# The opening of a hybrid attention and expert kernel: another order of loads, column products and table

## Chip, cores and metric

One core of one Trainium2 chip. The metric is the device time of one execution in microseconds; three runs of the kernel before gave 1021.66, 1022.80 and 1024.69, median 1022.8.

## The reference, cut to what matters

```python
def reference(x, c, w_ada, b_ada, norm_attn, ..., norm_final):
    mod = jnp.einsum('bd,lde->lbe', jax.nn.silu(c), w_ada) + b_ada[:, None, :]
    for l in range(DEPTH):                       # DEPTH = 1
        sh1, sc1, g1, sh2, sc2, g2 = jnp.split(mod[l], 6, axis=-1)
        h = modulate(rms_norm(x, norm_attn[l]), sh1, sc1)     # h*(1+scale)+shift
        x = x + g1[:, None, :] * hybrid_mixer(h, w_in[l], w_out[l], rel_bias)
        h = modulate(rms_norm(x, norm_ffn[l]), sh2, sc2)
        x = x + g2[:, None, :] * peer_ffn(h, peer_wq[l], peer_subkeys[l], peer_u[l], peer_v[l])
    return rms_norm(x, norm_final)
```

x is 256 rows of 1024 values; `w_ada` is 1024 x 6144, its six parts of 1024 columns are shift, scale and gate of the two halves (parts 0 to 5). `hybrid_mixer` projects h with one matrix to queries, keys and values of 16 heads and a small indexer, adds a bias of relative position, and takes softmax attention: 8 heads over a causal block, 8 heads over the keys that the indexer selects. `peer_ffn` is an expert layer with 16384 one-neuron experts.

## The kernel before, in words

x is held transposed: 8 tiles of 128 features by 256 tokens (`xT`). Products that need full precision are made from two halves of each operand, a rounded high part (ScalarE, L106) and the rest as low part (VectorE, L108), in three matmuls (`mm3`, L125 to L127). Weight tiles of 128x1024 (512 KB) come one after the other through four `raw` buffers (`load_next`, L94), in the order of the list `seq`; all loads are issued by SyncE. `take` gives out the next split tile, and `ahead` keeps loads and splits in front of it.

**The opening** (up to `start.close()`) stands in a region of manual schedule: there each engine issues its instructions, SyncE its DMAs too, in the order in which the code emits them. Behind it a scheduler orders the instructions by the order of emission and its own estimate of when they are ready; the order of the attention's parts is the string ORDER (A projects queries and keys of a pair of heads, S makes its scores and softmax, B multiplies with the values, I, N and T are the indexer's projections, norm and selection, V the second half of the values, Dk accumulates part k of `w_ada` and Ek makes its columns).

In the opening:
- SyncE loads small tables, x, two weight tiles, the 8 chunks of the scale part (part 1) of `w_ada` (L158), two weight tiles and the 8 chunks of the shift part (part 0), through 11 buffers, then the value tiles.
- ScalarE squares x (L236), TensorE sums over the features (L237), and VectorE with ScalarE makes rstd (L190 to L196).
- The scale vector is a product of silu(c) with 8 chunks of 128 rows. Chunks 0, 2 and 4 are multiplied on TensorE into rows (`ada_rows`, L300), copied (L303) and turned into columns by products with one value (L309). The other chunks are scaled and added on VectorE (`ada_dve`, L208 and L210), and `ada_end` (L317, L320) sums them over the partitions by products with a single column of ones, and adds the bias into `mod`. Products of ones with ones (`busy`, L257) are filler; their result is not used.
- `early_split` (L322) splits the first four weight tiles (two pairs of heads): two of them before rstd, two after `xh_all`.
- `xr_all` (L350) multiplies x by rstd; `xh_all` (L353 to L357) scales it into high part xh and low part xl. `early_mm` makes the projections of the first four tiles from them, still without the shift (96 products, L125 to L127), tiles 0 and 1 by turns of halves, then tiles 2 and 3.
- The shift vector (part 0) is accumulated wholly on VectorE in two halves of columns; after each half `ada_end`, and `sh_half` (L365 to L368) adds the shift to get h, as hh and hl. `early_shift` (L337) and `early_cols` (L342 to L345) make the correction of the early projections.
- `vproj_steps` (L274) multiplies four value tiles with h, each with the three products of `mm3`; the second half of them stands behind the opening.
- The bias of relative position: a one-hot product (L391), copied into `fr` (L394), written to DRAM (`frd`, L397, by SyncE behind all loads of `w_ada`), and read back as the table `bias` of 2 MB (L440) after `early_cols`, into a pool that takes the memory of the opening's weights.

After that A0 and A1 only copy the early projections out (L453), and S0 starts with scores (L494) and the sum with the bias (L504).

Of the kernel before, what the change touches and what calls it, by code (L numbers as in the profile page):

```python
# [7 lines left out]
FT = mybir.dt.float32  # L8
# [8 lines left out]
T = 256  # L17
# [14 lines left out]
NTAIL = 125  # L32
ORDER = "D2 S0 S1 I N B0 A2 T A3 B1 S2 D4 A4 S3 B2 E2 A5 S4 B3 A6 S5 E4 D3 A7 V B4 S6 B5 S7 B6 E3 B7"
EARLY = 4
BUSY0 = 13
BUSY1 = 2
BUSY2 = 4
ADA_PE = {(1, 0): (0, 2, 4), (1, 1): (0, 2, 4), (0, 0): (), (0, 1): ()}


@with_exitstack
def hybrid_kernel(ctx, tc, io, out):
# [11 lines left out]
    def bank(tag, bufs=1):  # L54
        return psum.tile([128, 512], FT, tag=tag, name=tag, bufs=bufs)
# [62 lines left out]

    def take():
        ahead(5, 3)  # L120
        at["use"] += 1
        return parts.pop(at["use"] - 1)
# [15 lines left out]
    start = ctx.enter_context(ExitStack())  # L138
    start.enter_context(tc.manual_schedule())
    w0_stack = ctx.enter_context(ExitStack())  # L140
    w0 = pool("w0", stack=w0_stack)
# [57 lines left out]
    def rows_rsqrt_steps(ps, n):  # L199
        r3 = [pf.tile([128, T], FT, tag="r3", name="r3", bufs=4) for _ in range(3)]  # L200
        return rsqrt_steps(ps[:, :T], *r3, 1.0 / n)

    def rows_rsqrt(ps, n):
        return list(rows_rsqrt_steps(ps, n))[1]

    def ada_step(acc, w, c, first):
# [8 lines left out]
    def ada_sum(part):  # L215

        acc = acc_tile()
        for c in range(8):
            ada_step(acc, ada_load(part, c), c, c == 0)
        return acc  # L220
# [13 lines left out]
    def square_sum(ms, x, c):  # L234
        sq = pf.tile([128, T], FT, tag="sq", name="sq", bufs=4)
        nc.scalar.activation(sq, x[:, c, :], AF.Square)  # L236
        nc.tensor.matmul(ms[:, :T], ones, sq, start=(c == 0), stop=(c == 7))  # L237
# [36 lines left out]
    def vproj_steps(g):  # L274
        pv = [bank_a() for _ in range(2)]
        for k in range(4):
            hi, lo = take()
            for c2 in range(2):
                c = 2 * k + c2
                w = slice(c2 * 512, c2 * 512 + 512)  # L280
                for tt in range(2):
                    ts = slice(tt * 128, tt * 128 + 128)
                    mm3(pv[tt], hh[:, c, ts], hl[:, c, ts], hi[:, w], lo[:, w], c == 0, c == 7)
            yield None
        for tt in range(2):
            nc.scalar.activation(v[:, tt, g * 512:(g + 1) * 512], pv[tt], AF.Copy)
# [7 lines left out]
    def ada_rows(part, half, box):  # L294
# [12 lines left out]
        for q in range(4):  # L307
            w = slice(q * 128, q * 128 + 128)
            nc.tensor.matmul(cols[:, q:q + 1], row[:, w], ones[0:1, 0:1], start=(q == 0),  # L309
                             stop=(q == 3 and len(chunks) == 8), skip_group_check=True)  # L310
        yield None

    def ada_end(part, half, cols):

        if len(ADA_PE[part, half]) < 8:
            for q in range(4):
                nc.tensor.matmul(cols[:, q:q + 1], (acc1 if part else acc0)[:, (half * 4 + q) * 128:(half * 4 + q + 1) * 128],  # L317
                                 ones[:, 0:1], start=(q == 0 and not ADA_PE[part, half]), stop=(q == 3), skip_group_check=True)
        s = slice(part * 8 + half * 4, part * 8 + half * 4 + 4)
        nc.vector.tensor_tensor(mod[:, s], cols[:, 0:4], bada[:, s], op=OP.add)  # L320

    def early_split():  # L322
        k = len(early_w)
        early_w.append(split(raws.pop(k), nc.vector, ehi[:, k, :], elo[:, k, :]))
        at["split"] += 1
        at["use"] += 1
# [19 lines left out]

    def xr_all():

        for c in range(8):
            nc.vector.tensor_tensor(xa[:, c, :], xT[:, c, :], rstd, op=OP.mult)  # L350

# [21 lines left out]

    box = {(1, 0): lambda: bank("c1")[:, 0:4], (1, 1): lambda: bank_a()[:, 4:8]}
    r10, r11 = ada_rows(1, 0, box), ada_rows(1, 1, box)
# [11 lines left out]
    for _ in range(3):  # L387
        next(r10)
        next(r11)
    fps = bank_a()  # L390
    nc.tensor.matmul(fps[:16, :256], rbT, oh, start=True, stop=True)  # L391
    fr = pf.tile([16, 384], FT, name="fr")
    nc.gpsimd.memset(fr, NEG)
    nc.scalar.activation(fr[:, :256], fps[:16, :256], AF.Copy)  # L394
    dp = pool("dp", space=bass.MemoryType.DRAM)
    frd = dp.tile([16, 384], FT, name="frd")
# [37 lines left out]

    at_stack = ctx.enter_context(ExitStack())
    pa = pool("pa", stack=at_stack)
    bias = pa.tile([128, 16, T], FT, name="bias")
    fa = frd[:]
    for g in range(2):
        nc.sync.dma_start(bias[:, 8 * g:8 * g + 8, :],  # L440
                          bass.AP(tensor=fa.tensor, offset=fa.offset + 8 * g * 384, ap=[[1, 128], [384, 8], [1, T]]))

# [15 lines left out]
    def proj_mm():  # L458
# [5 lines left out]
        return ps  # L464


# [81 lines left out]
    def indexer_norm():  # L548
        ik = IX["ik"]
        sq = pf.tile([128, T], FT, tag="sq", name="sq", bufs=4)  # L550
        nc.scalar.activation(sq[:64, :], ik[:64, :], AF.Square)
# [78 lines left out]
    for db in range(8):  # L630
        hi, lo = take()
        ps = bank_a()
        for c in range(8):
# [3 lines left out]
                                       op0=OP.mult, op1=OP.add)  # L637
        sq = pf.tile([128, T], FT, tag="sq", name="sq", bufs=4)
        nc.scalar.activation(sq, xT[:, db, :], AF.Square)
# [411 lines left out]
```

## Time and profile before

| | |
|---|---|
| median of 3 runs | 1022.8 us |
| the profiled execution's own time | 1022.12 us |
| its span in the trace | 1020.2 us |
| mean granted TensorE clock | 0.986 |
| TensorE busy | 979.2 us, 96% of the span |
| VectorE busy | 779.2 us, 76% |
| ScalarE busy | 634.8 us, 62% |
| DMA, mean over the span | 191 GB/s |

One execution is profiled; its trace lists each instruction with its start and duration, in microseconds from the span's start. PE is TensorE, PEld its loading of weights, DVE VectorE, ACT ScalarE, POOL GpSimd, SP SyncE; a q behind the name is the engine's instruction queue. Lnnn is the line of the kernel. An fp32 matmul shows as two passes. "[1.03 <-DVE s L505]" says that the engine stood idle 1.03 us before the instruction and what ended the wait. PEclk is the clock that TensorE was granted, as a share of 2.4 GHz.

### The profile page before, as it was taken

The numbers are of one execution on the slowest core, as the hardware profiler recorded it, in microseconds if no ns is written. First come the engines' busy times: TensorE is split into PE (matmuls) and PEld (weight loads), VectorE is DVE, ScalarE is ACT, GpSimd is POOL, SyncE is SP. The second block draws the span as 40 slices with busy tenths as digits, with TensorE's granted clock in tenths as the row PEclk, the third lists the DMA queues.
The fourth block names the chain that finished last, engine by engine and source line by source line (L and its number), as shares of the span: only waits on it lengthen the run. The fifth ranks groups of instructions, "written<-read, shape, count | busy, mean of one in ns | idle before, by whom it ended". The sixth has DMA issues, their size and how long they took to land.

```text
span 1020.2 us, 16221 instructions
## 1 busy us (share of the span) xinstructions
PE 979.2 (96%) x5691; PEld 832.9 (82%) x5691; DVE 779.2 (76%) x1601; ACT 634.8 (62%) x1419; POOL 20.8 (2%) x62
## 2 busy tenths in 40 slices
PE   8899799899899999999999999999999999999996
PEld 5768687899678788888888888887888888888885
DVE  5768996789999988888889898767555555555556
ACT  3556476455556599988988888544544555545443
POOL 0000010002100000000000000000000000000000
PEclk9799999999999999999999999999999999999999
DMA  8588574555356555555555555678665665565551
GB/s 347 214 288 301 157 245 140 170 173 162 122 165 187 173 178 165 166 166 166 166 168 168 164 169 167 216 254 283 210 198 191 190 199 189 193 199 188 199 191 63
DMA packets 54996, 195.15 MB, mean 191 GB/s; under 512 B 6097, under 2 KB 8193, under 8 KB 54530
## 3 DMA queue, kind: packets, MB, share of 16 engines
q1 hardware_dynamic: 54626, 192.80, 58.2%
q10 hardware_dynamic: 288, 1.31, 0.3%
q8 instruction: 45, 0.74, 0.3%
q14 instruction: 37, 0.30, 0.1%
HBM read 191.97 MB, written 2.12 MB: 190 GB/s over the span
## 4 chain that ended last, share of the span: by engine, by line
PE 62%; DVE 8%; DMA 2%; ACT 2%; issue 1%; DVEq 0%; ACTq 0%
PE c L898 11%; PE c L126 10%; PE c L125 10%; PE c L127 10%; PE pa L898 8%; PE c L899 6%; PE pa L899 4%; DVE lo L108 2%; PE pb L855 1%; PE pb L856 1%; DMA raw<-w_ada 1%; DMA raw<-V 1%; ACT hi L106 1%; DVE gt L905 1%; ACT ol L848 0%
## 5 line engine op out<-in xcount | busy, mean ns | idle before, releaser
L108 DVE TENSOR_TENSOR lo<-raw,hi 128x1024 fp32r<-128x1024 f32 x300 | 366.4, 1223 | 168.7 <-ACT hi L106 167.8
L106 ACT ACTIVATE hi<-raw 128x1024 fp32r<-128x1024 f32 x303 | 320.3, 1058 | 228.4 <-PE c L127 151.6
L898 PE MATMUL c<-h,hi 128*128 128x512 f32 x608 | 218.2, 399 | 1.2 <-ACT hi L106 1.2
L126 PE MATMUL c<-lo,w 128*128 128x512 f32 x509 | 198.6, 390 | 1.2 <-DVE lo L108 1.2
L125 PE MATMUL c<-hi,w 128*128 128x512 f32 x509 | 198.5, 390 | 0.0
L127 PE MATMUL c<-hi,w 128*128 128x512 f32 x509 | 197.9, 389 | 0.0
L899 PE MATMUL c<-h,lo 128*128 128x256 f32 x608 | 158.4, 281 | 5.1 <-DVE lo L108 5.1
L898 PE MATMUL pa<-h,hi 128*128 128x512 f32 x416 | 151.6, 399 | 1.0 <-ACT hi L106 1.0
L898 PEld LDWEIGHTS c<-h,hi 128*128 128x128 f32 x608 | 112.8, 188 | 22.7 <-ACT hi L106 2.1
L899 PEld LDWEIGHTS c<-h,lo 128*128 128x128 f32 x608 | 114.0, 189 | 12.7 <-DVE lo L108 7.3
L126 PEld LDWEIGHTS c<-lo,w 128*128 128x128 f32 x509 | 95.6, 188 | 23.1 <-DVE lo L108 3.4
L125 PEld LDWEIGHTS c<-hi,w 128*128 128x128 f32 x509 | 95.5, 188 | 20.5 <-ACT hi L106 0.8
L127 PEld LDWEIGHTS c<-hi,w 128*128 128x128 f32 x509 | 95.6, 188 | 19.8
L899 PE MATMUL pa<-h,lo 128*128 128x256 f32 x416 | 108.5, 281 | 1.1 <-DVE lo L108 1.1
L898 PEld LDWEIGHTS pa<-h,hi 128*128 128x128 f32 x416 | 78.0, 188 | 15.3 <-ACT hi L106 1.4
L848 ACT ACTIVATE ol<-og,glT 128x128 f16<-128x128 f16 x256 | 88.0, 435 | 0.0
L899 PEld LDWEIGHTS pa<-h,lo 128*128 128x128 f32 x416 | 78.1, 189 | 6.0 <-DVE lo L108 2.3
L125 PE MATMUL pa<-h,hi 128*128 128x256 f32 x240 | 71.0, 296 | 4.2 <-ACT h L246 3.1
L127 PE MATMUL pa<-h,lo 128*128 128x256 f32 x240 | 68.9, 289 | 3.6 <-DVE lo L108 3.6
L126 PE MATMUL pa<-h,hi 128*128 128x256 f32 x240 | 69.3, 289 | 0.0
L904 ACT ACTIVATE gt<-c 128x256 f32<-128x256 f32 x76 | 29.1, 382 | 35.9 <-PE c L898 35.6
L125 PEld LDWEIGHTS pa<-h,hi 128*128 128x128 f32 x240 | 46.9, 195 | 5.4 <-ACT h L246 3.3
(280 smaller groups left out, 1389.4 us busy)
## 6 DMA issues: line engine op xcount, KB each, us to landing
raw<-U SPq DMA_DIRECT2D x128, 512.0 KB, 3.5
raw<-V SPq DMA_DIRECT2D x128, 512.0 KB, 4.2
wada<-w_ada SPq DMA_DIRECT2D x40, 512.0 KB, 7.8
raw<-wqk SPq DMA_DIRECT2D x19, 512.0 KB, 6.1
raw<-wq SPq DMA_DIRECT2D x16, 512.0 KB, 3.7
raw<-wv SPq DMA_DIRECT2D x8, 512.0 KB, 5.0
raw<-wo SPq DMA_DIRECT2D x8, 512.0 KB, 4.2
raw<-w_ada SPq DMA_DIRECT2D x8, 512.0 KB, 4.7
```

The lines of the kernel that those rows point to most:

```text
L106: nc.scalar.activation(hi, raw, AF.Copy)
L108: lo_eng.tensor_tensor(lo, raw, hi.bitcast(FT), op=OP.subtract)
L125: nc.tensor.matmul(ps, lh, rh, start=first, stop=False)
L126: nc.tensor.matmul(ps, lh, rl, start=False, stop=False)
L127: nc.tensor.matmul(ps, ll, rh, start=False, stop=last)
L848: nc.scalar.activation(ol[:, q // 2, :, q % 2], og[:, q // 2, :, q % 2], AF.Copy, scale=glT[:, t0 + q:t0 + q + 1])
L855: nc.tensor.matmul(w[:, qs], o1[:, a, :, b], og[:, a, :, b], start=True, stop=False)
L856: nc.tensor.matmul(w[:, qs], o1[:, a, :, b], ol[:, a, :, b], start=False, stop=True)
L898: both = [lambda: nc.tensor.matmul(ps, hi[:, w], hcat[:, c].rearrange("p a t -> p (a t)"), start=(c == 0), stop=(c == 7)), lambda: nc.tens ...
L899: lambda: nc.tensor.matmul(ps[:, T:], lo[:, w], hh[:, c, :], start=False, stop=False)]
L904: nc.scalar.activation(gt, ps[:, T:], AF.Copy)
L905: nc.vector.tensor_tensor(gt, gt, ps[:, :T], op=OP.add)
```

## The change

The loads come in another order: the scale chunks first, then four weight tiles, the shift chunks (8 buffers instead of 11, so that each takes the place of a scale chunk), and two value tiles. The bias row's product and copy move ahead of the squares, and its write to DRAM is issued by ScalarE. rstd times x is two broadcast instructions, one between the accumulation steps and one behind them. The splits of the early weight tiles move behind the accumulation, and the early products go tile by tile. The column products of `ada_rows` and `ada_end` are 128 columns wide, of which one is read. Chunks 5 to 7 of the shift's second half become rows on TensorE. The value tiles' high parts are made before the shift's halves and their low parts behind them, and the value products of a tile do the high parts first. The bias table gets a pool of its own and is loaded within the opening, and three chunks of part 2 are loaded there. D2 stands behind S0, S1 and I in ORDER. The filler counts change, and two buffers go.

```diff
-ORDER = "D2 S0 S1 I N B0 A2 T A3 B1 S2 D4 A4 ..."
+ORDER = "S0 S1 I D2 N B0 A2 T A3 B1 S2 D4 A4 ..."
-BUSY1 = 2
-BUSY2 = 4
-ADA_PE = {(1, 0): (0, 2, 4), (1, 1): (0, 2, 4), (0, 0): (), (0, 1): ()}
+BUSY1 = 4
+BUSY2 = 5
+ADA_PE = {(1, 0): (0, 2, 4), (1, 1): (0, 2, 4), (0, 0): (), (0, 1): (5, 6, 7)}
...
-    load_next()
-    load_next()
     for part in (1, 0):
         for c in range(8):
-            w = first_w[part, c] = w0.tile([128, 1024], FT, tag="wada", name="wada", bufs=11)
+            w = first_w[part, c] = w0.tile([128, 1024], FT, tag="wada", name="wada", bufs=8)
...
         if part:
-            load_next()
-            load_next()
+            for _ in range(EARLY):
+                load_next()
+    for _ in range(2):
+        load_next()
...
-            hi, lo = take()
-            for c2 in range(2):
-                c = 2 * k + c2
-                w = slice(c2 * 512, c2 * 512 + 512)
-                for tt in range(2):
-                    ts = slice(tt * 128, tt * 128 + 128)
-                    mm3(pv[tt], hh[:, c, ts], hl[:, c, ts], hi[:, w], lo[:, w], c == 0, c == 7)
+            hi, lo = take(g > 0 or k > 1)
+            for term in range(2):
+                for c2 in range(2):
...
+                        if term == 0:
+                            nc.tensor.matmul(pv[tt], hh[:, c, ts], hi[:, w], start=(c == 0), stop=False)
+                            nc.tensor.matmul(pv[tt], hl[:, c, ts], hi[:, w], start=False, stop=False)
+                        else:
+                            nc.tensor.matmul(pv[tt], hh[:, c, ts], lo[:, w], start=False, stop=(c == 7))
...
-            nc.tensor.matmul(cols[:, q:q + 1], row[:, w], ones[0:1, 0:1], start=(q == 0),
-                             stop=(q == 3 and len(chunks) == 8), skip_group_check=True)
+            nc.tensor.matmul(cols[:, w], row[:, w], ones[0:1, :], start=(q == 0), stop=False, skip_group_check=True)
...
-                nc.tensor.matmul(cols[:, q:q + 1], (acc1 if part else acc0)[...],
-                                 ones[:, 0:1], start=(q == 0 and not ADA_PE[part, half]), stop=(q == 3), skip_group_check=True)
+            nc.tensor.matmul(cols[:, q * 128:q * 128 + 128], (acc1 if part else acc0)[...],
+                             ones, start=(q == 0 and not ADA_PE[part, half]), stop=(q == 3), skip_group_check=True)
...
+    def xr_half(half):
+        cs = slice(half * 4, half * 4 + 4)
+        nc.vector.tensor_tensor(xa[:, cs, :], xT[:, cs, :], rstd[:, None, :].to_broadcast([128, 4, T]), op=OP.mult)
...
     busy(BUSY0)
+    frd = bias_rows()
     for c in range(8):
         square_sum(ms, xT, c)
-    early_split()
-    early_split()
     rs = rows_rsqrt_steps(ms, D)
     next(rs)
     ada_dve(1, (1,), first=True)
     rstd = next(rs)
-    xr_all()
-    ada_dve(1, (3, 5, 6, 7))
+    ada_dve(1, (3,))
+    xr_half(0)
+    ada_dve(1, (5, 6, 7))
...
-    nc.sync.dma_start(frd, fr)
+    run(r10)
+    run(r11)
     busy(BUSY1)
-    run(r10)
-    busy(BUSY1)
-    run(r11)
-    busy(BUSY2)
+    xr_half(1)
+    early_hi(0)
+    early_hi(1)
+    early_lo(0)
     ada_end(1, 0, box[1, 0])
     ada_end(1, 1, box[1, 1])
+    busy(BUSY2)
     xh_all()
     early_ps = [bank_b(), bank_b(), bank("c0"), bank("c1")]
-    for half in range(2):
-        early_mm(0, half)
-        early_mm(1, half)
-    early_split()
-    early_split()
+    for k in range(EARLY):
+        if k:
+            if k > 1:
+                early_hi(k)
+            early_lo(k)
+        early_mm(k, 0)
+        early_mm(k, 1)
     xa_half(0)
     xa_half(1)
-    for k in (2, 3):
-        early_mm(k, 0)
-        early_mm(k, 1)
+    load_next()
+    load_next()
     ada_dve(0, range(8), slice(0, 512), first=True)
+    for _ in ADA_PE[0, 1]:
+        next(r01)
     ada_end(0, 0, bank("c2"))
+    hi_first(EARLY)
+    hi_first(EARLY + 1)
     sh_half(0)
-    ahead(6, 2)
-    ada_dve(0, range(8), slice(512, 1024), first=True)
+    lo_then(EARLY)
+    lo_then(EARLY + 1)
+    bias = bi.tile([128, 16, T], FT, name="bias")
...
+        nc.sync.dma_start(bias[:, 8 * g:8 * g + 8, :], ...)
+    there.update({(2, c): ada_load(2, c) for c in (2, 3, 4)})
+    ada_dve(0, [c for c in range(8) if c not in ADA_PE[0, 1]], slice(512, 1024), first=True)
     vg = vproj_steps(0)
     next(vg)
+    next(r01)
+    next(r01)
+    next(vg)
+    hi_first(EARLY + 2)
+    hi_first(EARLY + 3)
     shp = bank("c2")
     early_shift(0)
-    next(vg)
-    ada_end(0, 1, bank("c3"))
+    ada_end(0, 1, box[0, 1])
     sh_half(1)
+    lo_then(EARLY + 2)
+    lo_then(EARLY + 3)
     early_shift(1)
     early_cols()
```

`bias_rows` holds the lines L391 to L397 with `nc.scalar.dma_start`; `early_hi` and `early_lo`, and `hi_first` and `lo_then`, are the ScalarE and the VectorE instruction of a split as two calls. The buffers of `sq` and of the rsqrt rows go from 4 to 3.

## Rows read from the trace of the kernel before

**Rows 1.** The page's busy time and its clock in 40 slices.

```profile
PE 979.2 (96%) x5691; PEld 832.9 (82%) x5691; DVE 779.2 (76%) x1601; ACT 634.8 (62%) x1419; POOL 20.8 (2%) x62
...
PEclk9799999999999999999999999999999999999999
```

**Rows 2.** Stretches: length; busy PE, PEld, DVE, ACT, POOL; clock, DMA share, GB/s.

```profile
22.00:23.00 1.00, 1.00 (x9) 0.99 (x9) 0.96 (x2) 0.00 (x0) 0.00 (x0) 0.85 1.04 414
24.00:29.00 5.00, 4.28 (x22) 4.19 (x20) 0.49 (x3) 0.29 (x1) 0.00 (x0) 0.50 1.03 407
...
34.00:42.00 8.00, 8.00 (x69) 8.00 (x68) 7.02 (x10) 3.11 (x8) 0.00 (x0) 1.00 0.54 180
44.00:46.00 2.00, 0.00 (x0) 0.00 (x0) 1.66 (x5) 2.00 (x6) 0.00 (x0) 1.00 0.00 0
48.50:52.50 4.00, 4.00 (x11) 3.13 (x10) 3.86 (x6) 0.01 (x1) 0.00 (x0) 0.50 0.82 262
70.00:100.00 30.00, 28.20 (x209) 25.30 (x209) 26.86 (x49) 20.02 (x51) 0.00 (x0) 1.00 0.93 320
100.00:120.00 20.00, 13.96 (x95) 12.02 (x94) 18.11 (x67) 8.01 (x21) 2.25 (x4) 0.91 0.44 140
```

**Rows 3.** VectorE in order of time: start, duration, what, wait before it.

```profile
10.25 2.51 DVE L108 TENSOR_TENSOR elo<-raw,ehi 128x1024 fp32r<-128x1024 f32 x2 [6.68 <-ACT ehi L106]
12.68 0.42 DVE L190 TENSOR_SCALAR r<-c 128x256 f32<-128x256 f32 x1
13.09 0.75 DVE L208 TENSOR_SCALAR acc<-wada,sc 128x1024 f32<-128x1024 f32 x1
...
15.46 2.77 DVE L350 TENSOR_TENSOR xa<-xT,r 128x256 f32<-128x256 f32 x8
18.15 5.24 DVE L210 SCALAR_TENSOR_TENSOR acc<-wada,sc,acc 128x1024 f32<-128x1024 f32 x4
...
29.25 3.28 DVE L357 SCALAR_TENSOR_TENSOR xl<-xa,amul,xh 128x256 fp32r<-128x256 f32 x8 [0.58 <-ACT xh L356]
...
35.79 5.48 DVE L210 SCALAR_TENSOR_TENSOR acc<-wada,sc,acc 128x512 f32<-128x512 f32 x7
...
58.66 0.16 DVE L320 TENSOR_TENSOR mod<-c,small 128x4 f32<-128x4 f32 x1 [1.47 <-PE c L317]
...
70.42 0.42 DVE L504 SCALAR_TENSOR_TENSOR s<-pb,bias 128x256 f32<-128x256 f32 x1 [2.09 <-DMA bias<-frd]
```

**Rows 4.** TensorE in order of time: start, duration, what, wait before it.

```profile
6.73 3.72 PE L237 MATMUL c<-sq,ones 128*128 128x256 f32 x16 [0.34 <-ACT sq L236]
...
16.88 1.88 PE L300 MATMUL c<-wada,sc 128*1 128x512 f32 x4 [0.68 <-DMA wada<-w_ada]
18.69 0.60 PE L391 MATMUL pa<-oh,rbT 32*16 32x256 f32 x2
19.22 0.71 PE L257 MATMUL pb<-ones 128*128 128x128 f32 x4
...
26.43 1.84 PE L317 MATMUL pa<-ones,acc 128*128 128x1 f32 x8
29.27 0.58 PE L125 MATMUL pb<-xh,ehi 128*128 128x256 f32 x1 [0.99 <-ACT xh L356]
...
42.68 0.95 PE L317 MATMUL c<-ones,acc 128*128 128x1 f32 x8
46.67 0.80 PE L125 MATMUL pa<-hi,h 128*128 128x512 f32 x1 [3.03 <-ACT hi L106]
...
67.92 0.39 PE L127 MATMUL pa<-hi,h 128*128 128x512 f32 x1
...
71.09 0.92 PE L494 MATMUL pb<-kT,qT 64*128 64x256 f32 x4 [1.03 <-DVE s L505]
...
111.22 0.41 PE L127 MATMUL pa<-h,lo 128*128 128x256 f32 x1 [3.56 <-DVE lo L108]
```

**Rows 5.** ScalarE's queue issuing a DMA, near the kernel's end: start, duration, what.

```profile
1016.60 0.37 ACTq L991 DMA_DIRECT2D out_dram<-raw  x1
```

More of the change, by code (lines that the diff above doesn't have):

```diff
@@ L117, in ahead, with take @@
             at["split"] += 1
-    def take():
-        ahead(5, 3)
+    def take(look=True):
+        if look:
+            ahead(5, 3)
         at["use"] += 1
@@ L139, in hybrid_kernel @@
     start.enter_context(tc.manual_schedule())
+    at_stack = ctx.enter_context(ExitStack())
+    bi = pool("bi", stack=at_stack)
     w0_stack = ctx.enter_context(ExitStack())
@@ L199, in rows_rsqrt_steps @@
     def rows_rsqrt_steps(ps, n):
-        r3 = [pf.tile([128, T], FT, tag="r3", name="r3", bufs=4) for _ in range(3)]
+        r3 = [pf.tile([128, T], FT, tag="r3", name="r3", bufs=3) for _ in range(3)]
         return rsqrt_steps(ps[:, :T], *r3, 1.0 / n)
@@ L204, in rows_rsqrt @@
         return list(rows_rsqrt_steps(ps, n))[1]
+    there = {}
     def ada_step(acc, w, c, first):
@@ L218, in ada_sum @@
         for c in range(8):
-            ada_step(acc, ada_load(part, c), c, c == 0)
+            ada_step(acc, there.get((part, c)) or ada_load(part, c), c, c == 0)
         return acc
@@ L234, in square_sum @@
     def square_sum(ms, x, c):
-        sq = pf.tile([128, T], FT, tag="sq", name="sq", bufs=4)
+        sq = pf.tile([128, T], FT, tag="sq", name="sq", bufs=3)
         nc.scalar.activation(sq, x[:, c, :], AF.Square)
@@ L308, in ada_rows, with hi_first, lo_then, early_hi @@
             w = slice(q * 128, q * 128 + 128)
-            nc.tensor.matmul(cols[:, q:q + 1], row[:, w], ones[0:1, 0:1], start=(q == 0),
-                             stop=(q == 3 and len(chunks) == 8), skip_group_check=True)
+            nc.tensor.matmul(cols[:, w], row[:, w], ones[0:1, :], start=(q == 0), stop=False, skip_group_check=True)
         yield None
     def ada_end(part, half, cols):
-        if len(ADA_PE[part, half]) < 8:
-            for q in range(4):
-                nc.tensor.matmul(cols[:, q:q + 1], (acc1 if part else acc0)[:, (half * 4 + q) * 128:(half * 4 + q + 1) * 128],
-                                 ones[:, 0:1], start=(q == 0 and not ADA_PE[part, half]), stop=(q == 3), skip_group_check=True)
+        for q in range(4):
+            nc.tensor.matmul(cols[:, q * 128:q * 128 + 128],
+                             (acc1 if part else acc0)[:, (half * 4 + q) * 128:(half * 4 + q + 1) * 128],
+                             ones, start=(q == 0 and not ADA_PE[part, half]), stop=(q == 3), skip_group_check=True)
         s = slice(part * 8 + half * 4, part * 8 + half * 4 + 4)
[L320 to L324, printed above, removed]
+        nc.vector.tensor_tensor(mod[:, s], cols.rearrange("p (q k) -> p q k", q=4)[:, :, 0], bada[:, s], op=OP.add)
+    def hi_first(k):
+        hi = st.tile([128, 1024], FR, tag="hi", name="hi", bufs=3)
+        nc.scalar.activation(hi, raws[k], AF.Copy)
+        parts[k] = hi
+    def lo_then(k):
+        lo = st.tile([128, 1024], FR, tag="lo", name="lo", bufs=3)
+        nc.vector.tensor_tensor(lo, raws.pop(k), parts[k].bitcast(FT), op=OP.subtract)
+        parts[k] = (parts[k], lo)
+        at["split"] += 1
+    def early_hi(k):
+        nc.scalar.activation(ehi[:, k, :], raws[k], AF.Copy)
+    def early_lo(k):
+        nc.vector.tensor_tensor(elo[:, k, :], raws.pop(k), ehi[:, k, :].bitcast(FT), op=OP.subtract)
+        early_w.append((ehi[:, k, :], elo[:, k, :]))
         at["split"] += 1
@@ L372, in run, with bias_rows @@
             pass
-    box = {(1, 0): lambda: bank("c1")[:, 0:4], (1, 1): lambda: bank_a()[:, 4:8]}
-    r10, r11 = ada_rows(1, 0, box), ada_rows(1, 1, box)
+    def bias_rows():
+        fps = bank_a()
+        nc.tensor.matmul(fps[:16, :256], rbT, oh, start=True, stop=True)
+        fr = pf.tile([16, 384], FT, name="fr")
+        nc.gpsimd.memset(fr, NEG)
+        nc.scalar.activation(fr[:, :256], fps[:16, :256], AF.Copy)
+        dp = pool("dp", space=bass.MemoryType.DRAM)
+        frd = dp.tile([16, 384], FT, name="frd")
+        nc.scalar.dma_start(frd, fr)
+        return frd
+    box = {(1, 0): lambda: bank("c1"), (1, 1): bank_a, (0, 1): lambda: bank("c3")}
+    r10, r11, r01 = ada_rows(1, 0, box), ada_rows(1, 1, box), ada_rows(0, 1, box)
     busy(BUSY0)
+    frd = bias_rows()
     for c in range(8):
         square_sum(ms, xT, c)
-    early_split()
-    early_split()
     rs = rows_rsqrt_steps(ms, D)
@@ L432, in hybrid_kernel @@
     w0_stack.close()
-    at_stack = ctx.enter_context(ExitStack())
     pa = pool("pa", stack=at_stack)
[L437 to L441, printed above, removed]
     def rev(ap):
@@ L549, in indexer_norm @@
         ik = IX["ik"]
-        sq = pf.tile([128, T], FT, tag="sq", name="sq", bufs=4)
+        sq = pf.tile([128, T], FT, tag="sq", name="sq", bufs=3)
         nc.scalar.activation(sq[:64, :], ik[:64, :], AF.Square)
```

24 lines of the change are left out of this document (11 added, 13 removed).

## The prediction

> **What bounds the kernel now.** I read the page first. TensorE is busy 979.2 of 1020.2 us, and the slices show a granted clock under full speed in the first two fortieths [rows 1]. After 120 us it is busy in nearly every slice, so the change can win time in the opening alone (to about 68 us) and in the attention stage that follows on its heels. Next came the table of stretches [rows 2]. The DMA engines run full, at 407 to 414 GB/s, up to 29 us; the clock falls at 22 to 23 us although TensorE is busy in that whole microsecond, and is at the lower level, 1.2 GHz, from 24 to 29 us; it is back at 2.4 GHz from 34 to 42 us. From 44 to 46 us TensorE does nothing, and from 48.5 to 52.5 us it is again at half clock. Then the VectorE and TensorE timelines [rows 3, 4] give the chain that sets the opening's end: loads, square sum, accumulation of the scale part (its last of four steps ends at 18.15 + 5.24 = 23.39), column products (to 26.43 + 1.84 = 28.27), first early product (29.27), last xl (29.25 + 3.28 = 32.53), end of the early products, behind which the first shift columns stand at 42.68 (VectorE had their sum ready at 35.79 + 5.48 = 41.27), the second half's mod (58.66), the last value product (67.92). At 70.42 VectorE still waits 2.09 us for the bias table, and TensorE waits 1.03 us behind it at 71.09.
>
> **The change, part by part.** I re-timed the opening in the new order with the old durations; engines issue in program order there. No DMA is added or taken away.
>
> *Start.* The bias row's product and its copy move ahead of the squares. The product takes 0.60 us [rows 4], the copy of 256 columns about the 0.42 of VectorE's step of that width [rows 3], and its DMA is now issued by ScalarE: the one issue of that queue in the rows took 0.37 [rows 5]; as bounds I take 0.3 and 1.5 (ScalarE held until the copy is out). So the squares start near 7.9 instead of 6.3, and the square sum, 3.72 us on TensorE [rows 4], ends near 12.0 instead of 10.45. This is a loss of 1.5 on TensorE, but VectorE does not feel it: its first rsqrt step stood at 12.68 behind two low parts of 2.51 us [rows 3], which go later. It now starts at about 12.1.
>
> *Scale first.* Two weight tiles leave the front of the queue: 1 MB at 410 GB/s is 2.5 us, so the last scale chunk lands near 18.1. VectorE: rsqrt from 12.1, first chunk 0.75, three steps of 0.42 behind ScalarE's two, second chunk 5.24 / 4 = 1.31, half the x product, three more chunks of 1.31 [rows 3]. The half product is one broadcast instruction of 1024 elements, which the trace does not show; the low part of that size takes 2.51 / 2 = 1.25, four old products 2.77 / 2 = 1.39; I take 1.25, nearest in shape. The accumulation ends near 21.2, not 23.39. TensorE's row products, 1.88 us for four with the last one's tail, so about 0.43 apart [rows 4], run 12.0 to 17.2.
>
> *Wide columns.* Each group of four products (eight passes) gets 128 columns. The filler has just that shape: 0.71 us for four passes at full clock, so 1.42 for eight; the narrow ones took 0.95 at full clock and 1.84 at half [rows 4]. For the one-row form I bound it by 0.95 and 2.1 (the filler at half clock, near 0.26 a pass) and take 1.42. There are seven such groups, so TensorE pays about 0.47 x 7 = 3.3 us in work, in exchange for clock.
> The Trainium skill, page "TensorE: Matmul & The Clock Gate", section "Back-to-back issue gap", speaks against this part: it puts a product of up to 64 columns at about 60 cycles and one of 128 at 134. By that ratio eight wide passes would be an estimated 2.1 us and the seven groups would cost 8.2 instead of 3.3, which would leave the forecast at about 1021.4. The measured filler of the same shape decides: the ratio here is 1.5, because the load of the weights is in both.
>
> TensorE then: rows to 17.2, two column groups to 20.1, filler of eight passes to 21.5, two end groups to 24.4, mod at 24.6, ten filler passes to 26.2. First early product 26.2 instead of 29.27; xl runs from 25.4 to 28.7 instead of 32.53. **Gain 3.8.** The half x product and the first low part lie on VectorE between 21.2 and 23.7, under the end groups; without that cover they would cost 2.5.
>
> *Early products.* 69 of them start in 8 us at full clock, 0.12 each [rows 2]. There are 96, in the order of tiles. The first tile is fed by xl and done near 29.0; the second waits for its low part, now after xl on VectorE: 28.7 + 1.25 = 30.0, a new stall of 1 us. Then 72 products end near 38.6 instead of 42.8. **Gain 4.2.** The two other low parts (to 32.3) are ready in time.
>
> *First half of the shift.* VectorE's eight half chunks, 6.0 us (5.48 for seven [rows 3]), run 32.3 to 38.3. Three chunks of the second half are now six row passes on TensorE, 0.43 each, and stand ahead of the column products: 38.6 + 2.6 + 1.4 = 42.6. mod is there at 42.8 instead of 43.8 (42.68 + 0.95 and an add): **only 1.0 is kept.** But the high parts of two value tiles are now ready (before, TensorE waited 3.03 at 46.67 for one [rows 4]), so value products start near 43.4; the low parts follow hl at 46.4 and 47.6, a stall of about 1.
>
> *Second half.* VectorE has five half chunks, about 3.5 us, done near 51.1. TensorE does value tile one (to 47.3), the row's columns (48.7), tile two (51.5), four pairs of shift products (53.4), end group (54.8). mod near 54.9 instead of 58.8: **gain 3.9.** What stood behind it took 67.92 + 0.3 - 58.8 = 9.4 us before; the same work gives 64.0. **Gain 4.3 at the last value product.** The clock is taken as full throughout, as nothing longer than 1.3 us leaves TensorE idle.
>
> *Bias.* Its two loads go out near 32, behind weight tiles, into an own pool, and land before 46, where the DMA engines stood still. The waits at 70.42 and 71.09 go: **1.0 more.** What is late next is the sums' split in the attention.
>
> *Queues.* With eight slots, each shift chunk waits for the scale chunk before it; releases (13.7 to 21.2) come 1 to 2 us before the queue's turn (512 KB at 410 GB/s, 1.28 us a tile, from about 14 to 23), so nothing. POOL's memset stays where it was. SyncE's later loads wait for early low parts at 30.0 to 32.3; who needs them, the value tiles, comes at 35 and later. Fewer sq and r3 buffers: nothing, ScalarE runs ahead of TensorE in the squares as before.
>
> *Attention.* VectorE is ahead by more than TensorE when it starts (59.8 to 61 against 70.4). From 100 to 120 us TensorE is busy 13.96 of 20, with VectorE at 18.11 [rows 2], and waits 3.56 at 111.22 for a low part [rows 4]. Of this I book **1.0** as gained (bounds: 5 lost, 5 gained).
>
> Sum: 4.3 + 1.0 + 1.0 = 6.3 us. The profiled execution took 1022.1, so 1015.8; the median of the runs shown stands 0.7 higher, so **1016.5**.
>
> **Rivals.**
> (a) The clock falls again. In the trace it fell under busy narrow products, with no idle gap beside them; if the wide ones don't prevent that, the last column groups cost 0.26 instead of 0.18 a pass (26 passes, 2 us) and the early products start at half clock (some 1 to 2 us): 1019.5. For it: TensorE's row products stay one column wide in weights, and there is a new gap near 7 to 8.3 us.
> The Trainium skill's same page, section "HAM oscillation", lays falls to idle gaps between bursts; by that alone wider columns would change nothing. The fall at 22 to 23 us with full busy time [rows 2] shows that idle gaps are not all.
> (b) Slower. The order string puts the gate part's accumulation (D2) behind the indexer's projections. It is 0.75 + 7 x 1.31 = 9.9 us of VectorE work; before, it lay within 70 to 100 us, where TensorE was busy 28.20 of 30 us [rows 2]. If the scheduler sets it among the top-k selection and the low parts that TensorE waits for (111.22), each microsecond is paid. It decides from 6.3 us on; all 9.9 give 1026.
> (c) The lead is absorbed: VectorE is busy 26.86 of 30 us from 70 to 100 [rows 2]; if the selection ends no earlier than before, the opening buys nothing: 1021.8. Against it: VectorE itself starts nine us earlier.
> (d) More: the waits of 100 to 120 us shrink too, as VectorE's lead is larger than TensorE's: 1012.
>
> **How the numbers follow.** Forecast (1014 to 1019) 0.58; (a) 0.14, half of it within the bound; (b) 0.10; (c) 0.08; (d) 0.10. A measurement tells 0.3%, 3.1 us, from no change. Faster: 0.58 + 0.10 + 0.07 = 0.75; same 0.08 + 0.07 = 0.15; slower 0.10. The range 1011 to 1020.5 takes in forecast, (a) and (d), and leaves out (b) and (c), 0.18.
>
> **What would show it.** In the new profile: clock at full speed from 20 to 42 us; scale accumulation ended by 21.5; first early product near 26; their end near 38.6; mod's second shift half near 55; last value product near 64; no VectorE wait for the bias. Wrong if the clock drops before 30, if the early products end after 41, or if the wait that ends at 111.22 is less than 4 us earlier although the opening is.

## The result, and the profile after

The changed kernel took 1015.02 us (median of five runs, 1014.03 to 1016.78); the kernel before took 1021.66 on the same chip (five runs, 1019.27 to 1024.69). The ratio is 0.9938, 95% interval 0.9917 to 0.9958: 6.6 us faster in the medians. The forecast was 1016.5 (6.3 off a median of 1022.8), within 1011 to 1020.5. The two profiled executions stand 5.3 us apart (1022.12 and 1016.78, the slowest of the changed kernel's five), their spans 5.2 (1020.2 and 1015.0).

The page of the changed kernel, busy time and clock in 40 slices, against [rows 1]: the work is the same; the clock of the second slice (25 to 51 us) rises from 7 to 9 tenths, and that of the fifth (about 102 to 127 us) falls from 9 to 8.

```profile
PE 979.2 (96%) x5707; PEld 831.2 (82%) x5707; DVE 775.9 (76%) x1592; ACT 636.6 (63%) x1420; POOL 21.4 (2%) x62
...
PEclk9999899999999999999999999999999999999999
```

Stretches of the changed kernel, columns as in [rows 2]; the first and the last line are new:

```profile
20.50:23.50 3.00, 2.67 (x13) 2.37 (x12) 3.00 (x3) 1.06 (x1) 0.00 (x0) 0.50 1.04 414
24.00:29.00 5.00, 4.86 (x38) 4.60 (x38) 3.79 (x11) 4.01 (x9) 0.00 (x0) 1.00 1.02 406
34.00:42.00 8.00, 8.00 (x51) 5.62 (x51) 3.96 (x6) 2.12 (x2) 0.00 (x0) 1.00 1.06 375
44.00:46.00 2.00, 1.73 (x7) 1.07 (x7) 2.00 (x4) 1.90 (x4) 0.00 (x0) 1.00 1.03 403
48.50:52.50 4.00, 4.00 (x18) 2.64 (x19) 2.23 (x3) 0.00 (x0) 0.00 (x0) 1.00 0.55 198
70.00:100.00 30.00, 28.95 (x219) 25.90 (x218) 27.75 (x49) 17.68 (x39) 0.00 (x0) 1.00 0.87 287
100.00:120.00 20.00, 15.89 (x94) 13.17 (x94) 18.38 (x58) 8.52 (x21) 2.24 (x4) 0.83 0.49 165
109.00:115.60 6.60, 5.81 (x21) 4.20 (x21) 6.60 (x11) 3.10 (x10) 0.43 (x2) 0.50 0.54 160
```

The clock still falls to 1.2 GHz, which it is at from 20.5 to 23.5 us, but from 24 us it is back at 2.4 GHz, where [rows 2] show 0.50. The dead stretch from 44 to 46 us and the second fall at 48.5 are gone. In the attention, 109 to 115.6 us is at half clock; in the kernel before it was 111.4 to 114.9.

VectorE of the changed kernel in order of time, against [rows 3]:

```profile
12.51 0.43 DVE L193 TENSOR_SCALAR r<-c 128x256 f32<-128x256 f32 x1 [8.96 <-PE c L242]
16.38 1.22 DVE L373 TENSOR_TENSOR xa<-xT,r 128x1024 f32<-128x1024 f32 x1
17.52 3.92 DVE L215 SCALAR_TENSOR_TENSOR acc<-wada,sc,acc 128x1024 f32<-128x1024 f32 x3
24.60 0.16 DVE L329 TENSOR_TENSOR mod<-pa,small 128x4 f32<-128x4 f32 x1 [0.82 <-PE pa L325]
25.54 3.29 DVE L380 SCALAR_TENSOR_TENSOR xl<-xa,amul,xh 128x256 fp32r<-128x256 f32 x8 [0.58 <-ACT xh L379]
42.46 0.16 DVE L329 TENSOR_TENSOR mod<-c,small 128x4 f32<-128x4 f32 x1 [4.32 <-PE c L325]
54.20 0.16 DVE L329 TENSOR_TENSOR mod<-c,small 128x4 f32<-128x4 f32 x1 [3.40 <-PE c L325]
64.44 0.42 DVE L544 SCALAR_TENSOR_TENSOR s<-pb,bias 128x256 f32<-128x256 f32 x1 [0.77 <-PE pb L534]
```

TensorE of the changed kernel, against [rows 4]:

```profile
8.75 3.72 PE L242 MATMUL c<-sq,ones 128*128 128x256 f32 x16 [1.38 <-ACT sq L241]
12.40 5.31 PE L310 MATMUL c<-wada,sc 128*1 128x512 f32 x12
17.64 1.15 PE L319 MATMUL c<-ones,row 1*128 1x128 f32 x8
18.63 1.05 PE L319 MATMUL pa<-ones,row 1*128 1x128 f32 x8
...
21.49 2.08 PE L325 MATMUL c<-ones,acc 128*128 128x128 f32 x8 [0.33 <-DVE acc L215]
23.36 1.20 PE L325 MATMUL pa<-ones,acc 128*128 128x128 f32 x8
24.39 1.28 PE L262 MATMUL pb<-ones 128*128 128x128 f32 x10
...
38.60 2.73 PE L310 MATMUL c<-wada,sc 128*1 128x512 f32 x6
41.27 1.16 PE L325 MATMUL c<-ones,acc 128*128 128x128 f32 x8
43.32 0.50 PE L290 MATMUL pa<-hi,h 128*128 128x512 f32 x1 [0.89 <-ACT h L251]
...
62.48 1.07 PE L293 MATMUL pa<-lo,h 128*128 128x512 f32 x4
63.48 0.92 PE L534 MATMUL pb<-kT,qT 64*128 64x256 f32 x8
...
107.69 2.49 PE L534 MATMUL pb<-kT,qT 64*128 64x256 f32 x8 [2.56 <-DVE s L545]
```

The first scores start at 63.48, where they started at 68.24 before: 4.8 us. The end of the attention, VectorE's first residual add, comes at 176.10 before and 170.40 after: 5.7 us, so 0.9 more is won between. The next fences show that row, before and then after. From it to the end of the span it is 844.1 and 844.6 us: behind the attention nothing changed.

```profile
176.10 0.88 DVE L636 SCALAR_TENSOR_TENSOR xT<-pa,mod,xT 128x256 f32<-128x256 f32 x2 [0.60 <-PE pa L127]
```

```profile
170.40 0.88 DVE L676 SCALAR_TENSOR_TENSOR xT<-pa,mod,xT 128x256 f32<-128x256 f32 x2 [0.59 <-PE pa L128]
```

### The profile page after: what moved, and what is told of

It reads as the page before. It is cut to its first block, busy times and chain, and to the rows that moved or that the text cites. A ratio compares the mean times of both kernels' runs of the same rounds, so it can differ in the third digit from the quotient of the medians.

```text
span 1015.0 us, 16252 instructions
## 1 busy us (share of the span) xinstructions
PE 979.2 (96%) x5707; PEld 831.2 (82%) x5707; DVE 775.9 (76%) x1592; ACT 636.6 (63%) x1420; POOL 21.4 (2%) x62
## 4 chain that ended last, share of the span: by engine, by line
PE 62%; DVE 8%; DMA 2%; ACT 2%; issue 1%; DVEq 0%; ACTq 0%
PE c L938 11%; PE c L127 10%; PE c L126 10%; PE c L128 10%; PE pa L938 8%; PE c L939 6%; PE pa L939 4%; DVE lo L108 2%; PE pb L895 1%; PE pb L896 1%; DMA raw<-w_ada 1%; DMA raw<-V 1%; ACT hi L106 1%; DVE gt L945 1%; ACT ol L888 0%
## 5 line engine op out<-in xcount | busy, mean ns | idle before, releaser
L108 DVE TENSOR_TENSOR lo<-raw,hi 128x1024 fp32r<-128x1024 f32 x296 | 361.9, 1223 | 166.5 <-ACT hi L106 165.8
L106 ACT ACTIVATE hi<-raw 128x1024 fp32r<-128x1024 f32 x299 | 316.4, 1058 | 223.6 <-PE c L128 152.1
```

The source lines that it names most:

```text
L106: nc.scalar.activation(hi, raw, AF.Copy)
L108: lo_eng.tensor_tensor(lo, raw, hi.bitcast(FT), op=OP.subtract)
```

## The experiments

The opening is compared from VectorE's first rsqrt step to the first scores ("opening": 55.6 us before, 51.0 after), because the squares start between 7.0 and 8.6 us from one execution to another of nearly the same code. The attention is the time from the first scores to the residual add of the fences above (107.9 before, 106.9 after).

**The changed kernel again, as a control.**

> The changed kernel again, as the measure for its variants. Theory (the opening is one chain, and what it gains is carried one to one to the end): 1014 to 1016 us, early products end at 38.6 us, the last value product near 63.3, the out-projection's first residual add at 170.4. The granted clock fell at 20.6 us and was back at 24 in the profiled run; the theory says that it is back before the first early product (25.6) in any run. Rival (the clock is luck): the fall comes at another place or reaches into the early products, which then end later than 40.

1014.45 us, ratio 0.993 (0.9914 to 0.9946); opening 50.8, attention 106.8. The result repeats. The clock is at 1.2 GHz from 20 to 22 us and back before the first early product (25.06); the last one ends at 38.19.

**Narrow columns again.**

```diff
-nc.tensor.matmul(cols[:, w], row[:, w], ones[0:1, :], ...)
+nc.tensor.matmul(cols[:, q * 128:q * 128 + 1], row[:, w], ones[0:1, 0:1], ...)
-nc.tensor.matmul(cols[:, q * 128:q * 128 + 128], acc, ones, ...)
+nc.tensor.matmul(cols[:, q * 128:q * 128 + 1], acc, ones[:, 0:1], ...)
```

If the width is what brings the clock back, the early products end later than the control's and the time is longer.

> The changed kernel with the column products one column wide again (28 products, same result in the column that is read). [...] Rival (the width does nothing for the clock): early products end at 38.6 or up to 0.5 earlier, since eight wide passes took 1.15 to 1.20 us and narrow ones 0.95 to 1.05; the whole 1014 to 1015.

1016.99 us, ratio 0.9954 (0.9937 to 0.9972): 2.5 us above the control. The intervals of the ratios overlap a little, but each of its five runs (1016.32 and more) lies above all six of the control's (1016.24 and less). TensorE of this kernel:

```profile
21.28 1.84 PE L325 MATMUL pa<-ones,acc 128*128 128x1 f32 x8
22.98 2.48 PE L262 MATMUL pb<-ones 128*128 128x128 f32 x10
25.12 0.56 PE L126 MATMUL pb<-xh,ehi 128*128 128x256 f32 x1
...
27.61 0.37 PE L128 MATMUL pb<-xh,elo 128*128 128x256 f32 x1
27.81 0.28 PE L126 MATMUL pb<-xh,ehi 128*128 128x256 f32 x1
```

The ten filler passes take 2.48 us, not 1.28, and the first early products stand 0.21 us apart until 27.6: the clock falls at about the same place, but comes back 3 to 4 us later. Counted from the first rsqrt step the early products end 0.8 later and the first scores come 0.5 later (opening 51.3); the attention takes 108.4, 1.6 more, with a second stretch at half clock (123 to 127 us) that the control has not. In these two profiles width buys clock, and little of it is on the opening's path.

**Two weight tiles ahead of the scale chunks again.**

```diff
+    load_next()
+    load_next()
     for part in (1, 0):
...
-            for _ in range(EARLY):
+            for _ in range(EARLY - 2):
```

> The changed kernel with two early weight tiles loaded ahead of the scale chunks again; all else as changed. The last scale chunk then lands near 20.5 instead of 17.95. Theory: in the changed kernel VectorE's chain (square sum at 12.5, accumulation, 21.4) is the bound and hides most of it: accumulation ends near 21.9, row products at 18.5 instead of 17.6, early products 0.5 to 1 us later, 1015.5 to 1016. Rival (the load order is what the opening gains by): all 2.5 us are lost, accumulation ends near 23.9, early products end near 41, 1017.5.

1017.07 us, ratio 0.9952 (0.9936 to 0.9969): 2.6 us above the control by the medians, the intervals overlapping, and nearer to the rival's time than to the theory's. The profile bears out the theory's size: the accumulation ends 9.46 us after the first rsqrt step instead of 8.93; the opening takes 51.4, the attention 106.95. So the load order is worth 0.5 to 0.7 us in the opening. Another 1 us of this profile lies behind the attention, without a cause that I could point to, and what the rest of the 2.6 is stays open.

**D2 in its old place in ORDER, in the changed kernel, and its new place in the kernel before.**

```diff
-ORDER = "S0 S1 I D2 N B0 ..."
+ORDER = "D2 S0 S1 I N B0 ..."
```

> The changed kernel with the accumulation of the gate part (D2) first in the order of the attention again. Theory: its place is hidden work; the out-projection starts within 1 us of 170.4 and the whole is 1014 to 1016. Rival (the order of the attention gives or takes part of the result): the selection's start (97.0) and the TensorE wait near 102 to 107 move by 2 us or more, and the whole with them, 1012 or 1018.

> The kernel before with nothing but D2 behind S0, S1 and I in the order of the attention. With D2 first the changed kernel lost 3.0 us. Theory (the lead that the opening gives VectorE is taken up by D2 when it stands first, so its place pays only together with the earlier opening): 1020.5 to 1022. Rival (the place of D2 is a gain by itself): 1018.5, out-projection's first residual add near 173 instead of 176.1.

In the changed kernel the old place gives 1017.42 us, ratio 0.996 (0.9946 to 0.9973): 3.0 above the control, the intervals just touching. The profiled execution is the slowest of the nine (1021.95): its opening is 51.6, its attention 109.9 instead of 106.8, with a stretch at half clock (81 to 84.5 us) that no other version shows there. The stretch from 70 to 80 us, D2 in its old place and then as changed:

```profile
70.00:80.00 10.00, 7.51 (x59) 6.50 (x57) 10.00 (x17) 6.79 (x19) 0.00 (x0) 1.00 0.89 290
```

```profile
70.00:80.00 10.00, 9.80 (x79) 8.92 (x78) 9.50 (x11) 8.72 (x21) 0.00 (x0) 1.00 0.86 268
```

D2's accumulation steps stand between the first softmax steps, VectorE is busy throughout, and TensorE does 2.3 us less. In the kernel before, the new place alone gives 1023.07 us, ratio 1.0007 (0.9991 to 1.0024), with an attention of 109.7. By the medians the place of D2 counts only with the rest of the change; there it is a gain, and the idea that it lies hidden either way falls. How much of the 3.0 a usual execution loses in the attention this profile does not show.

**The bias table in the attention's pool and loaded behind the opening again.**

```diff
-    bi = pool("bi", stack=at_stack)
-    bias = bi.tile([128, 16, T], FT, name="bias")
...
     pa = pool("pa", stack=at_stack)
+    bias = pa.tile([128, 16, T], FT, name="bias")
```

> The changed kernel with the bias table back in the pool that takes the opening's memory, loaded behind the shift's correction; its write to DRAM stays early. Theory: TensorE's correction products end near 58.7, the 2 MB then need about 6 us, so the table lands near 65 to 66 while the first scores stand at 64.4; VectorE waits 1 to 2 us again and the whole loses 1 to 2: 1015.5 to 1016.5. Rival (another load order in the attention costs more than the wait): the weight tiles behind it are late too, 1018 or more. Rival (hidden): no change, 1014.5.

1020.7 us, ratio 0.9993 (0.9982 to 1.0005): nearly all of the gain is gone, 6.3 us above the control. VectorE and then TensorE of this kernel:

```profile
63.21 0.42 DVE L543 SCALAR_TENSOR_TENSOR s<-pb,bias 128x256 f32<-128x256 f32 x1 [2.65 <-DMA bias<-frd]
...
108.27 1.65 PE L533 MATMUL pb<-kT,qT 64*128 64x256 f32 x4 [3.67 <-DVE s L544]
```

The opening keeps its lead (50.0; the clock did not fall in it in this execution), and VectorE waits 2.65 us for the table, TensorE 0.66 behind it; but the attention takes 112.4, 5.6 more. The wait for the table is the smaller part. At 108 us TensorE waits 3.67 for a sum, where the changed kernel waits 2.56. And the clock falls a second time, from 123 to 130 us, where the changed kernel's does not; this kernel and then the changed one:

```profile
120.00:130.00 10.00, 8.31 (x32) 5.31 (x30) 8.29 (x21) 5.66 (x16) 1.84 (x4) 0.69 0.81 268
```

```profile
120.00:130.00 10.00, 9.14 (x68) 7.55 (x67) 6.67 (x20) 7.24 (x25) 2.26 (x4) 1.00 0.51 175
```

Of the 5.6, TensorE's longer busy time is 3.7 and its idle time 1.9. Whether the scheduler's order, the later weight loads or chance sets this was not taken apart.

**The bias row's product and DMA behind the squares.**

```diff
-    frd = bias_rows()
     for c in range(8):
         square_sum(ms, xT, c)
...
     next(rs)
+    frd = bias_rows()
     ada_dve(1, (1,), first=True)
```

> The changed kernel with the bias row's product, copy and DMA issue behind the square sum instead of ahead of it. Theory: in the changed kernel the squares wait for filler, bias product, copy and issue (start 7.96 and 8.28 in two profiles, 7.00 in a third, with x there at 6.2); here they start at 6.3, the square sum ends near 10.6, VectorE's accumulation ends near 19.8 instead of 21.1 to 21.4, the early products 1 to 1.6 us earlier, whole 1013. Rival (the loads set the pace, the last scale chunk lands at 17.95 either way): accumulation ends at 20.5 or later, and the whole stays at 1014.5.

1015.97 us, ratio 0.994 (0.9926 to 0.9954). The squares start at 6.29, the accumulation ends at 19.45 and the first scores come at 62.06, 0.9 before the control's; the attention takes 108.4, and the forecast of 1013 is missed. Its longest wait on TensorE is again one for a low part, as the 3.56 of [rows 4]:

```profile
104.70 0.58 PE L128 MATMUL pa<-h,lo 128*128 128x256 f32 x1 [3.95 <-DVE lo L108]
```

In this profile a microsecond won in the opening is no microsecond of the total.

**The shift wholly on VectorE again**, twice the same kernel, and once together with the bias row behind the squares.

```diff
-ADA_PE = {..., (0, 1): (5, 6, 7)}
+ADA_PE = {..., (0, 1): ()}
...
-    for _ in ADA_PE[0, 1]:
-        next(r01)
...
-    next(r01)
-    next(r01)
...
-    ada_end(0, 1, box[0, 1])
+    ada_end(0, 1, bank("c3"))
```

> The changed kernel with all shift chunks on VectorE again, none as rows on TensorE. Theory (a term that was sized wrong: the rows stand ahead of the first half's columns on TensorE and cost 2.7 us there): the first half's mod stands at 39.9 instead of 42.5, the second half's, now with 2.3 us more on VectorE, near 52 instead of 54.2; the whole is 2 us shorter, 1012.5. Rival (the rows are what brings the second half forward): VectorE ends the second half near 53 or later, mod at 55 to 56, the whole 1015.5 to 1016.5.

> The kernel with the whole shift on VectorE once more, beside the one with both edits. Theory: first scores 48.9 us behind the square sum again, attention 107.0, the whole 1013. Rival (its first timing was luck): 1014.5 to 1015.

> The changed kernel with both edits: the squares ahead of the bias row, and the whole shift on VectorE. Theory: the opening adds them up; counted from the square sum (near 10.5) the first scores stand 48.9 us later, at 59.5 to 60, three us before the changed kernel's. What the attention makes of it depends on the plan around the selection: with the changed kernel's 106.9 us from first scores to out-projection the whole is 1011, with the 108.4 of the run with squares first 1012.5. Rival (the scheduler's plan takes all of it, as it did with the squares first): 1014 or more.

The first measurement gives 1013.11 us, ratio 0.9909 (0.989 to 0.9927); the second 1013.74, 0.9927 (0.9899 to 0.9955); with the bias row behind the squares as well 1013.22, 0.992 (0.9898 to 0.9942). VectorE's mod of the shift's first half, in the first of them:

```profile
41.68 0.16 DVE L329 TENSOR_TENSOR mod<-c,small 128x4 f32<-128x4 f32 x1 [1.47 <-PE c L325]
```

It stands 0.9 us behind the last early product (40.75); in the changed kernel 3.8 (38.67 to 42.46), because the six row passes of 2.73 us go first on TensorE and VectorE waits 4.32 for them. The second half's mod then follows 12.0 us later instead of 11.7: the rows save 0.2 there and cost 2.9 ahead of it. The openings are 48.9 and 47.4 against 51.0, the attention the same (107.0 and 106.9). The 1.5 us between the two openings of one kernel is the clock: in the first it is at 1.2 GHz from 23.2 to 26.6 us, in the second it does not fall, and the 1.5 is there by the first early product (13.6 and 12.1 us behind the rsqrt step). In the medians this version is 1.3 to 1.9 us better than the changed kernel's 1015.02, 0.7 to 1.3 better than the control; the intervals overlap, so that the whole is better is likely and not shown. Its medians are the lowest here; moving the bias row adds nothing to it.

**The value tiles' high parts behind the first half of h.**

```diff
-    hi_first(EARLY)
-    hi_first(EARLY + 1)
     sh_half(0)
+    hi_first(EARLY)
+    hi_first(EARLY + 1)
```

> The changed kernel with the high parts of the first two value tiles made behind the shift's first half instead of ahead of it. Theory: what they buy is the clock: TensorE then stands idle for 3 us (42.4 to 45.4) as in the kernel before, is at 1.2 GHz for some 5 to 6 us after it, and the first scores come 2.5 to 3.5 us later, near 66; the whole 1017 to 1018. Rival (only the wait itself counts, and the low parts limit anyway): the clock holds and the first scores come 0.5 us later, 1015.

1019.63 us, ratio 0.9972 (0.9954 to 0.9989): 4.6 us above the changed kernel by the medians, 3.5 by the ratios. TensorE:

```profile
44.87 0.50 PE L290 MATMUL pa<-hi,h 128*128 128x512 f32 x1 [3.04 <-ACT hi L333]
```

The old wait for a high part is back, 3.04 instead of the 0.89 for h. The clock held all the same (1.00 from 24 to 62 us), so the theory's price, half clock behind the wait, did not come; and the low parts' waits shrink, so the second half's mod comes at 54.69 and the opening takes 51.8, 0.8 more, near the rival's 0.5. The attention takes 108.9, 2.0 more; again a low part is its longest wait. That is 2.8 us of it, and the time is above what either expected; the profiles, of which the changed kernel's shows its slowest execution, do not place the rest.

**The old amounts of filler.**

```diff
-BUSY1 = 4
-BUSY2 = 5
+BUSY1 = 2
+BUSY2 = 4
```

> The changed kernel with the old amounts of filler: two ones products (four passes) behind the rows' columns instead of four (eight passes), and four (eight passes) behind the end groups instead of five (ten); all else is as changed. Theory: the filler lies beside VectorE's accumulation and its xh and is on no chain, so the scale part's accumulation ends at the same place after VectorE's first rsqrt step (8.9 us), the first scores stay within 0.5 us of the changed kernel's by the same measure (51.0 us after that step), and the time is the changed kernel's within 2 us, 1013.5 to 1016.5. Rival: the filler is what keeps or brings back the clock; then the clock is still at its lower level when the early products start, their first ones take 0.21 us apart instead of 0.12, their end comes 1 to 2 us later, and the time is 1016.5 to 1018.

1016.49 us, ratio 0.9942 (0.9923 to 0.9961), at the border of the two ranges; the opening is 51.7, 0.7 more. TensorE:

```profile
21.35 2.08 PE L325 MATMUL c<-ones,acc 128*128 128x128 f32 x8 [1.03 <-DVE acc L215]
23.21 1.91 PE L325 MATMUL pa<-ones,acc 128*128 128x128 f32 x8
24.92 1.92 PE L262 MATMUL pb<-ones 128*128 128x128 f32 x8
26.49 0.48 PE L126 MATMUL pb<-xh,ehi 128*128 128x256 f32 x1
26.81 0.28 PE L127 MATMUL pb<-xl,ehi 128*128 128x256 f32 x1
```

Both end groups run at half clock, and mod comes at 25.16 instead of 24.60, 0.7 later counted from the first rsqrt step. From their second on the early products are at full clock. The rival is right in kind and its price half: the filler is worth about 0.7 us, in the end groups. The time is 1.5 us above the changed kernel's and 2.0 above the control's, the intervals overlapping.

## Why the prediction was right, and where it was not

**Start and scale first: right.** The square sum ended at 12.5 (forecast 12.0), VectorE's rsqrt started at 12.51 (12.1), the accumulation ended at 21.44 (21.2); the half x product took 1.22 (1.25). The part was named after the load order, but putting the order back cost only 0.5 us at the accumulation's end (2.6 in the medians). VectorE's chain, which starts at the late square sum, binds: in every other version of the changed kernel the accumulation ended 8.9 us after the first rsqrt step, whether that stood at 10.5 or at 14.0. In the kernel before it ended 10.7 us after that step; of the 1.8 between them 1.55 is the x product (2.77, now 1.22).

**Wide columns: the size and the clock both missed, with opposite signs.** The groups were booked at 1.42 us, the 0.71 of four filler passes doubled, which counts the end of the last pass twice (eight such passes took 1.16 at full clock in the run with narrow columns). At full clock the wide groups took 1.05 to 1.16, against 0.95 for the narrow ones [rows 4], so seven cost at most about 1.1 us more, not 3.3. The Trainium skill's page "TensorE: Matmul & The Clock Gate", section "Back-to-back issue gap", whose ratio would have made them 2.1, is further off: the rows show 1.1 to 1.2 times. The Trainium skill gives these cycles for isolated products, and says in the same section that in a stream the load of the weights and the product set the pace together. "The clock is taken as full throughout" failed: it fell at 20.5, so the first end group took 2.08 and the second 1.20. The two errors cancel by luck, and mod stood at 24.60 where 24.6 was forecast. By its own words the prediction was wrong if the clock drops before 30; it dropped, one group took 0.7 us more than booked, and it came back before the early products. Rival (a) had the event and not the price: it asked 3 us, and the two executions of the shift on VectorE, one with a fall and one without, stand 1.5 apart at the first scores.

**Early products and shift: right in place, one part with the wrong sign.** The early products ended at 38.67 (38.6), the first mod stood at 42.46 (42.8), the second at 54.20 (54.9), the last value product ended at 63.55 (64.0). The prediction saw that of 4.2 us "only 1.0 is kept" at the first mod, and still counted the three chunks on TensorE as a part of the gain. Its last sum there has a slip: 54.9 and 9.4 are 64.3, a gain of 3.9 and not 4.3; measured were 63.55, and 4.8. Its step "VectorE has five half chunks" moved work off an engine that was not the bound between the two mods: without it the opening is 2.1 us shorter where the clock falls in both, and the kernel 1 to 2 us by the medians.

**Bias: right that the wait goes, far too small.** 1.0 was booked, as the wait in [rows 4]. The loads went out at 32.6 and the first landed at 42.3, as forecast, and VectorE's first sum waits for scores, not for the table. Undone in the changed kernel the part costs 6.3. The stall that comes back with it is little changed (VectorE 2.65 where it was 2.09, TensorE 0.66 where it was 1.03); what its old length did not tell is that another attention follows it, with more time at half clock.

**Attention: 1.0 booked, next to none beyond the bias.** From the first scores to the residual add 0.9 was won, and the bias wait of 1.0 lies in it: TensorE idles 1.4 us less and is busy 0.5 longer. The wait that ended at 111.22 is replaced by one that ends at 107.69, 3.5 us earlier and 1.0 shorter: less than the 4 us that the prediction asked, and by its own words a sign of being wrong too. More time at half clock stands against it (6.6 us from 109; the clock of 100 to 120 us is 0.83, before 0.91 [rows 2]). Rival (b) looked in the right place with the wrong sign: D2 behind the indexer is worth 3 us by the medians. Rival (c) did not come, as the lead reached the residual add; nor did (d) in the total, as 100 to 120 us shows TensorE 1.9 us busier, but at a lower clock.

**The sum.** In the profiles 4.8 us came by the first scores, 0.9 in the attention, and 0.5 was lost behind: 5.2 of the 6.3; in the medians 6.6. The attention of the versions here took between 106.7 and 112.4 us for the same work in slightly different order and timing. That spread is nearly as large as the whole gain. In each profile it splits into TensorE's busy and idle time of that stretch, in us:

| | attention | busy | idle | time at half clock, about |
|---|---|---|---|---|
| before | 107.9 | 99.0 | 8.8 | 3 |
| changed | 106.9 | 99.5 | 7.4 | 7 |
| squares first | 108.4 | 99.2 | 9.1 | 7 |
| D2 first | 109.9 | 101.4 | 8.4 | 10 |
| table late | 112.4 | 103.3 | 9.1 | 14 |

The attention with the squares first is longer by TensorE's idle time; the two longest are longer mostly by its busy time, and they have the most of it at half clock. The 7 us more of the last row would lengthen work by an estimated 3.5 us, half of their length, where its busy time is 3.8 longer. Why TensorE waits where it does (for a low part in some, for a sum in others), and why the clock falls once or twice, is not shown. That the total came near the forecast, with terms off in both directions, is in part luck.

## What to carry to other kernels

Where a scheduler orders the next stage, price an early start and a moved load by a run, since the same microsecond in the opening gave between none and all of itself at the attention's end. Work moved to another engine pays only if the engine that it leaves ends last in that very stretch; six row passes in front of a column product cost 2.9 us there and saved 0.2. And the length of a wait in the old profile is not its price once all that stands ahead of it moves up: the table's 1.0 was worth 6.3 here, most of it in the stage behind.

## What the runs showed of the hardware that was not expected

- The clock fell to 1.2 GHz between 20 and 20.5 us in the changed kernel as between 22 and 23 before, behind row products, column products and filler. The Trainium skill's page "TensorE: Matmul & The Clock Gate", section "HAM oscillation", lays falls to idle gaps; the row of the microsecond in which it fell, in the changed kernel, shows TensorE without one:

```profile
20.00:21.00 1.00, 1.00 (x7) 0.86 (x6) 0.96 (x2) 0.79 (x2) 0.00 (x0) 0.62 1.01 401
```

With narrow columns, and with the old amounts of filler, it came back later (between 27 and 28, and between 26 and 27 us, where the changed kernel's was back by 24).
- The fall is not bound to the instructions alone. In two executions, the second one with the shift on VectorE and the one with the table late, the clock did not fall at all in the opening. The first and then the second execution of the shift on VectorE, the same kernel, each 10 us behind its first rsqrt step (14.00 and 11.91):

```profile
24.00:25.00 1.00, 1.00 (x7) 1.00 (x6) 1.00 (x2) 0.00 (x0) 0.00 (x0) 0.50 1.03 406
```

```profile
22.00:23.00 1.00, 1.00 (x12) 1.00 (x10) 1.00 (x1) 0.01 (x1) 0.00 (x0) 1.00 1.03 410
```

Nor is it bound to an idle gap: behind 3.03 us of idle TensorE at 46.67 us the kernel before ran at half clock; behind the 3.04 us of the version with the high parts late it did not.
- The square sum took 3.72 us in the changed kernel, and 5.41 in one execution of the version with the shift on VectorE:

```profile
8.55 5.41 PE L242 MATMUL c<-sq,ones 128*128 128x256 f32 x16 [1.41 <-ACT sq L241]
```

The granted clock there is 1.00 up to 9 us, 0.76 from 9 to 10 and 0.50 from 10 to 12: it fell under the square sum. That is 1.7 us on the opening's chain from the clock alone, in a kernel that was nonetheless among the fastest.
